# Regrouping the matmuls of a chunked RWKV-7 recurrence: keys' products as one block, outputs in two blocks

## The chip, the cores and the metric

The kernel runs on one core of a Trainium2 chip. Times are device microseconds (us) of that core; smaller is better. A time is given as the median of several runs. The profile is one further execution, taken by the hardware profiler: it lists every instruction of every engine with its start and length.

## The reference, cut to what matters

One layer of a hybrid decoder: a normed and modulated input goes through one projection, whose columns feed sparse attention (8 heads of 64) and an RWKV-7 time mix (8 heads of 64); both are concatenated and go through an output projection and a feed-forward network. There are 1024 prompt tokens and 8 sample tokens. The part that is changed here is the time mix of the prompt:

```python
def wkv7_step(S, inp):
    r, w, k, v, kk, a = inp
    sa = jnp.einsum('bhij,bhj->bhi', S, -kk)
    S = S * w[:, :, None, :] + sa[..., None] * (kk * a)[:, :, None, :] + v[..., None] * k[:, :, None, :]
    return S, jnp.einsum('bhij,bhj->bhi', S, r)
...
s_fin, ys = lax.scan(wkv7_step, s0.astype(jnp.float32), xs)
```

A state of 64 x 64 per head is carried from token to token; every token decays it, corrects it along one direction, adds value times key, and reads it with r. What comes out is group-normed, gets a bonus and a gate.

## The kernel before

The time mix is computed in chunks of C = 64 tokens. A unit of work is a pair of heads over QT = 256 tokens, so four chunks (HC = 4), and there are 16 units: unit n handles quarter q = n // 4 of the tokens and pair p = n % 4. A unit goes through four generators: `rw_prep` (operands), `rw_pre` (masked products within the chunks and the start of the inverses of the 32 x 32 diagonal blocks, which GpSimd computes), `rw_solve` (corrections, then the state chain) and `rw_norm` (outputs, group norm, gate). Each generator is cut by `yield` into steps, and `rwkv` gives each step a round: a unit starts every NR = 9 rounds, the steps of `rw_pre` come 9 to 14 rounds after the unit's start, those of `rw_solve` at RS = 27 to 35, those of `rw_norm` at RN = 36, 37, 39, 41 and 43. `rw_run` emits the steps sorted by round, so four or five units overlap.

The inverses of a unit go over DRAM: `rw_pre` writes the masked products `ga` to `d_l` (line 982), reads them back as `la` (986), GpSimd works on them in 31 pairs of instructions (1021 and 1023), `inv_back` writes `arr` to `d_t` (1034), behind the next unit's read of `la` on the SP queue, and reads the blocks `tt` (1038), which the first product of `rw_solve` (1052) uses.

At the end of `rw_solve` the state chain goes over the four chunks. For each head of the pair (e = 0 on partitions 0 to 63, e = 1 on 64 to 127) one matmul of the keys `bkt` with `uv` (line 1093, contraction over 128 partitions, 64 stationary columns, 64 moving columns) and one of the matrix `M` with the state `S` (line 1095, contraction over 64 partitions) add up in PSUM, and ScalarE scales the sum by `ec` into the next state (helper `SC`, line 51). The outputs in `rw_norm` add, for each chunk and head, the state part `Sa` by `rho` (line 1123, 64 partitions) and the chunk part `uv` by `gr` (line 1124, 128 partitions). In the first quarter (q = 0) the first chunk has no state, so the products with it fall away. All these are fp32 matmuls, which stand in the trace as two records each.

Attention of the prompt, the output projection of the first half of the tokens and the first feed-forward blocks are interleaved with the recurrence. The framework's planner sets the order on each engine ahead of time with a simulation of its own; on the chip every engine takes its instructions in that order.

Of the kernel before, what the change touches and what calls it, by code (L numbers as in the profile page):

```python
# [7 lines left out]
F32 = mybir.dt.float32  # L8
# [10 lines left out]
NS = 8  # L19
# [20 lines left out]
# rounds of the steps of a unit of the recurrence after its start; rounds from a unit's start to the next one's  # L40
# [19 lines left out]
# buffers: values; queries and keys; probabilities, transposed; keys split; queries loaded  # L60
# [13 lines left out]
class Ring:  # L74
    """tiles of several pools in turn"""
# [9 lines left out]
class Kern:  # L85
# [8 lines left out]
    # ------------------------------------------------------------------ constants  # L94
    def consts(self, ctx):
        nc, tc, I = self.nc, self.tc, self.I
        cp = self.cp
        with tc.tile_pool(name="tri0", bufs=1) as pp:
# [5 lines left out]
            self.tri_s = cp.tile([128, 128], F32, name="c_ts")     # col > row  # L104
# [25 lines left out]
        # parameters, one row of 128 each, transposed to columns  # L130
# [23 lines left out]
    # ------------------------------------------------------------------ adaLN modulation  # L154
# [17 lines left out]
    def mod_chunk(self, j, cw, wpool, tpool, keep=None):  # L172
        """columns cw*j.. of silu(c) @ w_ada; keep: SBUF tile [128, cw] taking the four partial rows"""
# [22 lines left out]
    # ------------------------------------------------------------------ norm 1, h transposed and split  # L196
# [5 lines left out]
    def norm_T(self, pool, mp, xp, fp):  # L202
        """norm 1 and its modulation; returns h transposed, hi, lo [128, KD, NT] (float32r)"""
# [55 lines left out]
    # ------------------------------------------------------------------ weights  # L259
    def wload(self, src, c0, n, wp):  # L260
        """src [1024, cols] -> hi, lo [128, KD, n], n <= 128"""
        return self.wtile(src, 0, c0, KD, n, wp)

    def mm_fm(self, ps, n, w, wc, m, h, t0, kd=KD):
        """ps[:m, :n] = W^T h (features by tokens), three passes"""
# [8 lines left out]
    def mm_tm(self, ps, n, h, t0, m, w, wc, kd=KD):  # L274
        """ps[:m, :n] = h^T W (tokens by features)"""
# [7 lines left out]
    # ------------------------------------------------------------------ RWKV, feature-major preparation  # L283
# [73 lines left out]
    def rsqrt(self, x, n, pool):  # L357
        """x [128, n] -> x ^ -0.5"""
# [12 lines left out]
    def rstd_tm(self, sq, blk, eps, floor, tp):  # L371
        """sq [128 = (2, 64), QT] -> (per token and half: sum with the weights of blk) ^ -0.5, tokens on partitions"""
# [11 lines left out]
    def rows_fm(self, ps, rn, n):  # L384
        """columns (token tile, half) of rn, tokens on partitions, as rows on all 64 partitions of each half"""
        for t in range(n):
            for h in range(2):
                self.nc.tensor.matmul(ps[64 * h:64 * h + 64, 128 * t:128 * t + 128],  # L388
                                      bc(rn[:, 2 * t + h:2 * t + h + 1], [128, 64]), self.ident, start=True, stop=True)

    def rw_prep(self, u, tp):
        """alpha, rho and kappa, beta of a pair of heads over QT tokens, per chunk; v; bonus"""
# [61 lines left out]
    # ------------------------------------------------------------------ indexer  # L454
    def idx_keys(self, h, wp, tp, sp, kp):
        """indexer keys, normalised, doubled over both halves of the partitions and split; weights per head"""
# [110 lines left out]
    def idx_select(self, tp, sp, smp):  # L567
        """scores -> 0 for the selected keys, -BIG for the others"""
# [17 lines left out]
        # keys under the middle: counted on DVE; on ACT as (under) - (over)  # L586
# [36 lines left out]
    def bis_open(self, lo, hi, w, t):  # L623
        """raise hi strictly over the maximum; w = hi - lo"""
# [7 lines left out]
    def bis_close(self, lo, hi, w, t):  # L632
        """the band of scores that rounding cannot tell from the threshold: [lo, hi]"""
# [7 lines left out]
    # ------------------------------------------------------------------ indexer of the sample tokens  # L641
    def smp_scores(self, tp, sp):
        nc, I = self.nc, self.I
        # page rows of 16 keys: row = page * 8 + sub; partition = (page of 16, sub of 8), column = (sequence, half)
# [14 lines left out]
        # head weights of every sequence on all partitions  # L659
# [7 lines left out]
        # head weights on partitions (eight times 16 heads), a column for each time  # L667
# [9 lines left out]
        # block-diagonal queries: column (key of two, head)  # L677
# [6 lines left out]
        # score of the token itself  # L684
# [15 lines left out]
        # cached keys  # L700
# [44 lines left out]
    def smp_prefix(self, x, rs, out, tp):  # L745
        """x [128, 16, 16] 0/1: inclusive count in the order (half, partition, key) of every sequence; totals"""
# [17 lines left out]
    def smp_select(self, tp, sp, dp):  # L764
# [56 lines left out]
        nc.vector.tensor_scalar(t, cnt, -1.0, TOPK + 0.5, op0=OP.mult, op1=OP.add)      # places left, + 0.5  # L821
# [11 lines left out]
        # slot of every selected key: the token itself, when selected, has slot 0  # L833
# [12 lines left out]
        # row of the key in the pools, selected ones only  # L846
# [35 lines left out]
    # ------------------------------------------------------------------ queries, keys, values (tokens on partitions)  # L882
    def split_sample(self, hi, lo, pool, name):
        """the sample tokens of a split operand as stationary columns: high parts at 0, low parts at 64"""
# [7 lines left out]
    def mm_smp(self, hs, w, wc, n, tp, out):  # L892
        """out [NS, n] = sample tokens times the n columns of w from wc"""
# [55 lines left out]
    # ------------------------------------------------------------------ RWKV recurrence: a pair of heads, QT tokens  # L949
    def rw_pre(self, u, tp, dp):  # L950
        """masked products within the chunks; starts the inverses"""
# [4 lines left out]
        # [.., 1, :]: V (tokens on partitions 0..63) and, later, the corrections without state (64..127);  # L956
        # [64.., .., 0, :]: what the state adds to the corrections
# [955 lines left out]
```

## Time and profile before

| | |
|---|---|
| runs | 2125.37, 2136.69, 2147.43 us; median 2136.69 |
| span of the profiled execution | 2141.3 us |
| TensorE matmul busy | 2033.1 us, 95% |
| VectorE busy | 1201.5 us, 56% |
| ScalarE busy | 815.7 us, 38% |
| GpSimd busy | 791.6 us, 37% |

The profiled execution's own time is its span, from the first instruction to the last. PE is TensorE's matmul, PEld its weight load, DVE VectorE, ACT ScalarE, POOL GpSimd, SP the engine that issues DMAs. Ends of matmuls are modelled, starts are measured; so a matmul's price is best read from the starts of two neighbours. A shape such as 128*64 128x64 says that the stationary operand has 128 rows and 64 columns, and that the operand named last has 128 partitions and 64 columns.

### The profile page before, as it was taken

The numbers are of one execution on the slowest core, as the hardware profiler recorded it, in microseconds if no ns is written. First come the engines' busy times: TensorE is split into PE (matmuls) and PEld (weight loads), VectorE is DVE, ScalarE is ACT, GpSimd is POOL, SyncE is SP. The second block draws the span as 40 slices with busy tenths as digits, with TensorE's granted clock in tenths as the row PEclk, the third lists the DMA queues.
The fourth block names the chain that finished last, engine by engine and source line by source line (L and its number), as shares of the span: only waits on it lengthen the run. The fifth ranks groups of instructions, "written<-read, shape, count | busy, mean of one in ns | idle before, by whom it ended". The sixth has DMA issues, their size and how long they took to land.

```text
span 2141.3 us, 38397 instructions
## 1 busy us (share of the span) xinstructions
PE 2033.1 (95%) x14794; PEld 1738.6 (81%) x14794; DVE 1201.5 (56%) x2904; ACT 815.7 (38%) x1650; POOL 791.6 (37%) x1381
## 2 busy tenths in 40 slices
PE   5999999889978999999999999999999999999998
PEld 3887888789964667777777887877788889999998
DVE  7777988997466554565565453575344463121215
ACT  5466676423222334455444332222322232222221
POOL 3411345332452246555635520101311244545452
PEclk8999999999988787999999899999999999999999
DMA  7311234233166654222113521443633234323333
GB/s 254 84 30 30 61 114 119 70 95 106 59 199 192 168 144 102 72 57 63 42 47 96 132 87 45 142 125 96 177 92 101 80 119 138 99 79 99 91 98 110
DMA packets 303206, 220.28 MB, mean 103 GB/s; under 512 B 67151, under 2 KB 281650, under 8 KB 303022
## 3 DMA queue, kind: packets, MB, share of 16 engines
q1 hardware_dynamic: 298140, 200.99, 32.5%
q0 software_dynamic: 4864, 16.78, 2.5%
q8 instruction: 117, 1.92, 0.4%
q14 instruction: 67, 0.55, 0.1%
q10 hardware_dynamic: 18, 0.04, 0.0%
HBM read 187.11 MB, written 30.13 MB: 101 GB/s over the span
## 4 chain that ended last, share of the span: by engine, by line
PE 68%; DMA 4%; DVE 3%; issue 1%; POOL 1%; ACT 0%; SPq 0%; DVEq 0%; POOLq 0%; ACTq 0%
PE ps L270 26%; PE ps L1657 11%; PE ps L1546 4%; PE ps L1255 2%; PE ps L1244 2%; PE ps L1124 2%; PE ps L972 1%; PE ps L1093 1%; PE ps L1123 1%; PE ps L1095 1%; PE ps L1224 1%; PE ps L388 1%; PE ps L183 1%; PE ps L1052 1%; PE ps L1065 1%
## 5 line engine op out<-in xcount | busy, mean ns | idle before, releaser
L1621 POOL TENSOR_TENSOR fl<-fr,fh 128x1024 fp32r<-128x1024 f32 (+1 forms) x109 | 264.2, 2429 | 323.4 <-ACT fh L1620 321.2
L1620 ACT ACTIVATE fh<-fr 128x1024 fp32r<-128x1024 f32 (+1 forms) x183 | 190.9, 1055 | 481.2 <-PE ps L270 268.4
L270 PE MATMUL ps<-h2hi,fh 128*128 128x264 f32 (+2 forms) x1056 | 336.3, 320 | 1.2 <-ACT fh L1620 1.2
L270 PE MATMUL ps<-h2lo,fh 128*128 128x264 f32 (+2 forms) x1056 | 336.2, 320 | 0.0
L270 PE MATMUL ps<-h2hi,fl 128*128 128x264 f32 (+2 forms) x1056 | 332.7, 320 | 0.6 <-DVE fl L1621 0.6
L270 PE MATMUL ps<-h1hi,fh 128*128 128x344 f32 (+1 forms) x752 | 250.1, 333 | 2.0 <-ACT rl L556 1.3
L270 PE MATMUL ps<-h1lo,fh 128*128 128x344 f32 (+1 forms) x752 | 246.9, 328 | 0.0
L270 PE MATMUL ps<-h1hi,fl 128*128 128x344 f32 (+1 forms) x752 | 246.4, 328 | 0.0
L270 PEld LDWEIGHTS ps<-h2hi,fh 128*128 128x128 f32 x1056 | 198.8, 188 | 16.5 <-ACT fh L1620 3.7
L1021 POOL TENSOR_TENSOR itmp<-la,arr 128x24 f32<-128x24 f32 (+23 forms) x496 | 131.2, 265 | 218.6 <-DMA la<-d_l 182.5
L270 PEld LDWEIGHTS ps<-h2hi,fl 128*128 128x128 f32 x1056 | 197.6, 188 | 15.4 <-DVE fl L1621 1.8
L270 PEld LDWEIGHTS ps<-h2lo,fh 128*128 128x128 f32 x1056 | 198.9, 188 | 13.6 <-issue 0.3
L1646 DVE TENSOR_TENSOR fa<-fa,ps 128x256 f32<-128x256 f32 (+1 forms) x66 | 33.8, 512 | 255.0 <-PE ps L270 255.0
L1657 PE MATMUL ps<-al,fh 128*128 128x512 f32 (+2 forms) x528 | 166.0, 320 | 3.2 <-DVE al L1648 3.2
L1668 DVE TENSOR_TENSOR acc<-acc,ps 128x512 f32<-128x512 f32 (+2 forms) x224 | 107.9, 514 | 99.5 <-PE ps L1657 99.4
L1657 PE MATMUL ps<-ah,fh 128*128 128x512 f32 (+2 forms) x528 | 157.5, 322 | 3.6 <-DVE fa L1646 1.9
L1657 PE MATMUL ps<-ah,fl 128*128 128x512 f32 (+2 forms) x528 | 160.5, 320 | 0.0
L270 PEld LDWEIGHTS ps<-h1hi,fh 128*128 128x128 f32 x752 | 143.8, 191 | 8.3 <-ACT rl L556 3.4
L1621 DVE TENSOR_TENSOR fl<-fr,fh 128x1024 fp32r<-128x1024 f32 x74 | 92.6, 1256 | 101.7 <-ACT fh L1620 100.2
L1023 POOL TENSOR_TENSOR arr<-arr,itmp 128x24 f32<-128x24 f32 (+23 forms) x496 | 132.5, 267 | 38.0
L270 PEld LDWEIGHTS ps<-h1lo,fh 128*128 128x128 f32 x752 | 143.6, 191 | 2.4 <-issue 2.1
L270 PEld LDWEIGHTS ps<-h1hi,fl 128*128 128x128 f32 x752 | 143.5, 191 | 2.5 <-issue 2.5
(937 smaller groups left out, 4382.3 us busy)
## 6 DMA issues: line engine op xcount, KB each, us to landing
fr<-in_w_ffn_gate_dram SPq DMA_DIRECT2D x44, 512.0 KB
fr<-in_w_ffn_up_dram SPq DMA_DIRECT2D x44, 512.0 KB
fr<-in_w_ffn_down_dram SPq DMA_DIRECT2D x44, 512.0 KB
fr<-in_w_in_dram SPq DMA_DIRECT2D x34, 512.0 KB
wr<-in_w_ada_dram SPq DMA_DIRECT2D x8, 1024.0 KB
la<-d_l SPq DMA_DIRECT2D x16, 512.0 KB
fr<-in_w_out_dram SPq DMA_DIRECT2D x16, 512.0 KB
d_x<-X SPq DMA_DIRECT2D x14, 512.0 KB
```

Of the source, the lines that this page charges most:

```text
L270: mm = nc.tensor.matmul(ps[:m, :n], a[:, k, wc:wc + m], b[:, k, t0:t0 + n], start=(k == 0 and i == 0), stop=(k == kd - 1 and i == 2))
L1021: ie.tensor_tensor(t3, bc(la[:, s, s + 1:][:, None, :], [128, nu, nt]), bc(arr[:, 0:nu, s:s + 1], [128, nu, nt]), op=OP.mult)
L1023: ie.tensor_tensor(arr[:, 0:nu, s + 1:], arr[:, 0:nu, s + 1:], t3, op=OP.subtract)
L1124: nc.tensor.matmul(ys, uv[:, c, e, 1, :], gr[:, c, e, :], start=not st, stop=True)
L1244: nc.tensor.transpose(ps[:, 128 * (l % 4):128 * (l % 4) + 128], P[e][:, 128 * l:128 * l + 128], ident)
L1255: nc.tensor.matmul(po[o, 0:128], vt[:, l, o], PT[e][:, 128 * (l % 4):128 * (l % 4) + 128], start=(l == 0), stop=(l == i))
L1546: nc.tensor.matmul(p3[:, t, :], a[:, k, ts], b[:, k % 4, :], start=(k == 0 and n == 0), stop=(k == KD - 1 and n == 2))
L1620: nc.scalar.activation(hi, raw, AF.Copy)
L1621: self.loe.tensor_tensor(lo, raw, hi.bitcast(F32), op=OP.subtract)
L1646: nc.vector.tensor_tensor(a, a, pu[:, :n], op=OP.mult)
L1657: nc.tensor.matmul(ps[:, :n], a[:, 0, 128 * o:128 * o + 128], b[:, c:c + n], start=(i == 0), stop=(i == 5))
L1668: nc.vector.tensor_tensor(a, a, ps[:, :n], op=OP.add)
```

## The change

In `rw_solve` the products M and rho are computed in one step. In the next step the keys' products of all four chunks run as one block of 8 matmuls into one PSUM tile, and VectorE multiplies them by `ec` into the new tile `bu`. The state chain keeps only the products with M; VectorE scales each and adds the chunk's part of `bu` in one instruction. The first chunk is in that same step, so that the chain ends one step earlier. In `rw_norm` the state parts of all chunks come first and the chunk parts of all chunks after them, as one accumulation over the PSUM tile. The rest of the diff takes comments out.

```diff
     def rw_solve(self, u, tp):
...
         nc.vector.tensor_tensor(M, c4(ps[:, :QT]), bc(self.id2[:, None, :], [128, HC, C]), op=OP.add)
-        yield
         ps = new()
...
         nc.vector.tensor_tensor(rho, rho, c4(ps[:, :QT]), op=OP.add)
+        yield
+
+        bu = tp.tile([128, HC, C], F32, name="bu", bufs=2)
+        ps = new()
+        for c in range(HC):
+            for e, o in enumerate(E2):
+                nc.tensor.matmul(ps[o, 64 * c:64 * c + 64], bkt[:, c, o], uv[:, c, e, 1, :], start=True, stop=True)
+        nc.vector.tensor_tensor(bu, c4(ps[:, :QT]), bc(ec[:, :, None], [128, HC, C]), op=OP.mult)
+
         Sa = u.Sa = tp.tile([128, HC, C], F32, name="Sa", bufs=2)
         S = None
         if u.q:
             S = Sa[:, 0, :]
             nc.scalar.activation(S, self.sfin[:, u.p, :], AF.Copy)
         for c in range(HC):
+            Sn = Sa[:, c + 1, :] if c < HC - 1 else self.sfin[:, u.p, :]
+            if S is None:
+                nc.scalar.activation(Sn, bu[:, c, :], AF.Copy)
+            else:
+                ps = self.psc.tile([128, 512], F32, name="ps")
+                for e, o in enumerate(E2):
+                    nc.tensor.matmul(ps[o, 0:64], M[o, c, :], S[o, :], start=True, stop=True)
+                nc.vector.scalar_tensor_tensor(Sn, ps[:, 0:64], ec[:, c:c + 1], bu[:, c, :], op0=OP.mult, op1=OP.add)
+            S = Sn
             yield
-            Sn = Sa[:, c + 1, :] if c < HC - 1 else self.sfin[:, u.p, :]
-            ps = self.psc.tile([128, 512], F32, name="ps")
-            for e, o in enumerate(E2):
-                nc.tensor.matmul(ps[o, 0:64], bkt[:, c, o], uv[:, c, e, 1, :], start=True, stop=S is None)
-                if S is not None:
-                    nc.tensor.matmul(ps[o, 0:64], M[o, c, :], S[o, :], start=False, stop=True)
-            SC(nc, Sn, ps[:, 0:64], ec[:, c:c + 1])
-            S = Sn
         if u.q == T // QT - 1:
             self.wkv_out(u.p, tp)
...
     def rw_norm(self, u, tp):
...
         ps = new()
+
+        c0 = 0 if u.q else 1
+        E2 = [(e, slice(64 * e, 64 * e + 64)) for e in range(2)]
+        for c in range(c0, HC):
+            for e, o in E2:
+                nc.tensor.matmul(ps[o, 64 * c:64 * c + 64], Sa[o, c, :], rho[o, c, :], start=c == c0, stop=False)
         for c in range(HC):
-            for e in range(2):
-                o = slice(64 * e, 64 * e + 64)
-                ys = ps[o, 64 * c:64 * c + 64]
-                st = u.q or c
-                if st:
-                    nc.tensor.matmul(ys, Sa[o, c, :], rho[o, c, :], start=True, stop=False)
-                nc.tensor.matmul(ys, uv[:, c, e, 1, :], gr[:, c, e, :], start=not st, stop=True)
+            for e, o in E2:
+                nc.tensor.matmul(ps[o, 64 * c:64 * c + 64], uv[:, c, e, 1, :], gr[:, c, e, :], start=False, stop=c == HC - 1)
         nc.scalar.activation(y, ps[:, :QT], AF.Copy)
```

## Rows read from the trace of the kernel before

**Rows 1.** Stretches: us, busy PE PEld DVE ACT POOL, granted clock, DMA, GB/s

```profile
850.00:1150.00 300.00, 299.81 (x2876) 226.74 (x2876) 172.51 (x658) 144.55 (x351) 158.46 (x600) 0.98 0.21 54
1150.00:1200.00 50.00, 47.97 (x436) 37.31 (x432) 25.55 (x73) 21.68 (x47) 28.63 (x97) 0.83 0.57 159
1200.00:1350.00 150.00, 148.50 (x1103) 122.78 (x1102) 68.61 (x147) 47.43 (x98) 29.42 (x93) 0.95 0.26 80
```

**Rows 2.** The chain of waits, 780 to 1350 us, shares by line

```profile
by line: PE ps L1546 8.3%; PE ps L1255 6.9%; PE ps L270 6.2%; PE ps L1124 6.0%; PE ps L1244 5.4%; PE ps L1093 5.4%; PE ps L1123 5.3%; PE ps L1095 5.2%; PE ps L972 5.0%; PE ps L1224 4.0%; PE ps L388 3.5%; PE ps L1052 3.3%; PE ps L1065 3.3%; 
```

**Rows 3.** TensorE's groups by form, 780 to 1350 us: busy, mean, idle before

```profile
L1124 PE MATMUL ps<-gr,uv 128*64 128x64 f32 x256 | 43.2, 259 | 0.0
L1093 PE MATMUL ps<-uv,bkt 128*64 128x64 f32 x256 | 42.4, 248 | 2.8 <-ACT Sa L51 2.8
...
L1074 PE MATMUL ps<-bkt,uv 64*64 64x64 f32 x256 | 13.1, 226 | 0.2
```

**Rows 4.** TensorE's timeline, outputs of a first-quarter unit: start, us, instruction

```profile
875.85 0.34 PE L1124 MATMUL ps<-gr,uv 128*64 128x64 f32 x4
876.11 0.32 PE L1123 MATMUL ps<-rho,Sa 64*64 64x64 f32 x2
876.37 0.33 PE L1124 MATMUL ps<-gr,uv 128*64 128x64 f32 x2
```

**Rows 5.** TensorE's timeline, 1012.8 to 1018 us

```profile
1012.86 0.60 PE L997 MATMUL ps<-c_id,ar 128*64 128x128 f32 x4
1013.29 0.51 PE L377 MATMUL ps<-c_bm,t 128*128 128x2 f32 x4
...
1016.39 0.66 PE L388 MATMUL ps<-c_id,rn 128*64 128x128 f32 x8
1016.98 0.68 PE L1080 MATMUL ps<-gr,uv 64*64 64x64 f32 x16
1017.59 0.66 PE L1244 MATMUL ps<-c_id,P 128*128 128x128 f32 x4
```

**Rows 6.** VectorE's groups by form, 780 to 1350 us

```profile
L367 DVE SCALAR_TENSOR_TENSOR rq_a<-rq_y,rn 128x4 f32<-128x4 f32 x87 | 13.9, 161 | 1.4
...
L1137 DVE SCALAR_TENSOR_TENSOR y<-y,prm,ps 128x256 f32<-128x256 f32 x16 | 7.6, 478 | 12.6 <-PE ps L388 12.3
...
L1075 DVE TENSOR_TENSOR M<-ps,c_id 128x256 f32<-128x256 f32 x16 | 6.7, 421 | 3.2 <-PE ps L1074 2.8
```

**Rows 7.** Line 51, the state's scaling on ScalarE, and its idle before it

```profile
L51 ACT ACTIVATE Sa<-ps,ec x48: 293/314/316, 796.7 to 1328.0; 128x64 f32<-128x64 f32 x48
L51 ACT ACTIVATE sfin<-ps,ec x16: 314/314/316, 802.4 to 1333.4; 128x64 f32<-128x64 f32 x16
...
  PE ps L1095: 73.5, 49
```

**Rows 8.** Timelines of TensorE, GpSimd and SP: one unit's inverses

```profile
1007.56 1.16 PE L972 MATMUL ps<-ar,bk 64*128 64x128 f32 x8
...
1020.01 0.48 POOL L1021 TENSOR_TENSOR itmp<-la,arr 128x31 f32<-128x31 f32 x1 [7.88 <-DMA la<-d_l]
...
1040.77 0.20 POOL L1023 TENSOR_TENSOR arr<-arr,itmp 128x4 f32<-128x4 f32 x1
...
1042.73 0.63 SPq L1034 DMA_DIRECT2D d_t<-arr  x1
1049.35 1.73 SPq L1038 DMA_DIRECT2D tt<-d_t  x4
...
1060.64 1.09 PE L1052 MATMUL ps<-X,tt 64*64 64x128 f32 x16
```

**Rows 9.** Line 972 from 850 to 1110 us: 16 records per unit

```profile
L972 PE MATMUL ps<-ar,bk x144: 272/272/373, 855.8 to 1106.0; 64*128 64x128 f32 x144
```

**Rows 10.** ScalarE's timeline ahead of the output projection

```profile
1186.43 1.06 ACT L1517 ACTIVATE h2hi<-fr 128x1024 fp32r<-128x1024 f32 x1 [4.46 <-DMA fr<-d_mix]
...
1192.72 1.06 ACT L1620 ACTIVATE fh<-fr 128x1024 fp32r<-128x1024 f32 x1 [1.45 <-DMA fr<-in_w_out_dram]
```

## The prediction

> **What bounds the kernel now.** The recurrence lies between about 790 and 1335 us, so I read that part only. First the busy time by stretch [rows 1]: TensorE is busy 299.8 of 300 us from 850 to 1150, 48.0 of 50 and 148.5 of 150 after it, while VectorE has 172.5, ScalarE 144.6 and GpSimd 158.5 of the 300. The granted clock is 0.98 there, so nearly all of it runs at 2.4 GHz. Then the chain of waits from 780 to 1350 [rows 2]: it names TensorE's own lines and hardly anything else, and the four lines that the change regroups, 1093 and 1095 (state chain), 1123 and 1124 (outputs), hold 5.4 + 5.2 + 5.3 + 6.0 = 21.9% of 570 us, 124.8 us. Third, the groups by form [rows 3]: line 1093 waited for the state for 2.8 us in all. So TensorE is not kept waiting; a microsecond taken off its queue here is a microsecond of the end, until something else becomes late. Behind 1350 us the kernel is feed-forward, bound by TensorE too, and is only moved forward.
>
> Why these lines are dear is seen in the groups and the timeline. Line 1124 takes 43.2 us for 256 records, line 1074, with the same 64 moving columns and as many records, 13.1 us [rows 3]. (One fp32 matmul leaves two records.) In the timeline [rows 4] the output's matmuls alternate between a stationary tile of 128 rows (1124) and one of 64 rows (1123), and each change starts 0.26 us after the one before: 875.85, 876.11, 876.37. The first row is telling: four records, both heads, took the same 0.26 us as two, because both heads have the same tile shape. Where the shape stays [rows 5], line 1080 runs 16 records in 17.59 - 16.98 = 0.61 us, 0.076 us per matmul instead of 0.26.
>
> **The change part by part.** The number of matmuls stays: 128 keys' products, 120 state products, 120 state parts of outputs, 128 chunk parts, 496 in all. Only their order and grouping change.
>
> Removed: the alternation. 496 x 0.26 = 129 us agrees with the 124.8 us of the chain, which I take.
>
> Put in its place, per row durations: the keys' products, 16 blocks of 8 matmuls, all 128 x 64. The trace has no block of that shape with 64 moving columns. Bounds: from below line 1080's 0.61 us [rows 5]; from above no overlap of the two heads, priced below. Line 388 is nearer, because it has the same tile shape and alternating heads with 128 moving columns: 8 records in 0.59 us. Line 1124's four records in 0.26 us show the overlap at 64 columns. So 0.61: 16 x 0.61 = 9.8 us. Chunk parts of the outputs: the same shape, 16 x 0.61 = 9.8 us. State parts: 64 x 64, 12 blocks of 8 and 4 of 6 (first quarter), 12 x 0.61 + 4 x 0.49 = 9.3 us. State chain: a pair of heads per chunk stands alone between other work, 60 x 0.26 = 15.6 us. Sum 44.5 us; saved 124.8 - 44.5 = 80 us.
>
> A page speaks against the 32 blocks of 128 rows. The row: four records in the time of two [rows 4]. The Trainium skill, "TensorE: Matmul & The Clock Gate", section Part 3, The mechanism, says that a weight load overlaps matmuls in flight only where the row group differs; here both heads use all rows. By the row the blocks cost 0.61 us, by the rule about what the second rival below says; the row contradicts it for two heads.
>
> Evictions: the keys' products add 16 VectorE multiplications, near line 1075 (0.42 us) [rows 6], 6.7 us. The scaling of the state moves from ScalarE (64 of 0.31 us, 20 us [rows 7]) to VectorE; the trace has no such operation at 64 columns; its bounds are the 0.16 us of 4 columns and the 0.48 us of 256 [rows 6]; by the columns 0.24 us, 60 x 0.24 = 14 us. VectorE gets 21 us more in 545, which its idle 42% [rows 1] covers; uncovered it is 21 us on the path. Behind these operations on VectorE stand the masked scores and copies that attention's next matmuls need. I take 5 us, from 0 to 21. The four copies that stay on ScalarE are free: it loses more than it gets.
>
> Moved: M and rho now stand in one round, the chain starts in the fifth and ends one round before the unit's last. The outputs start at the same round, so they gain slack. No DMA is moved past anything by the code; only the last state transposition keeps its place. The extra PSUM tile per unit lies in a ring of three that its VectorE eviction empties in 0.4 us: nothing, or a wait of that length 16 times, 7 us.
>
> What is late next, first: the inverses. For one unit [rows 8] line 972 starts at 1007.6, GpSimd works from 1020.0 to 1041.0, the write back is issued at 1042.7, the read at 1049.4 to 1051.1, and the solve (1052) starts at 1060.6: 53.1 us, of which 9.6 lie behind the issue of the last read. Nine units' line 972 lie between 855.8 and 1106.0 [rows 9], 31.1 us per unit. The chain in the program has fixed rounds, so the 53.1 us shrink with the period: 31.1 - 5.0 (80/16) = 26.1, and 53.1 x 26.1 / 31.1 = 44.6 us. The latency needs 43.5 us up to the last read's issue, 41.7 when the write back no longer stands behind the next unit's read (1.8 us after GpSimd's end), and its landing, which no row gives: between 0 and the 7.0 us that write back and its wait take (1042.7 to 1049.4, rounded up). So a unit stalls 0 to 4 us, 12 units 0 to 48. The read is of small blocks, so I take 8 us in sum.
>
> Second: before the output projection TensorE has only recurrence work, while ScalarE waits for loads (4.46 and 1.45 us, up to 1192.7 [rows 10]). What is saved there is partly lost: 0 to 10, I take 6.
>
> Sum: 80 - 5 - 8 - 6 = 61 us. The profiled span, 2141.3 us, becomes 2080; it is 4.6 us over the runs' median, 2136.7, and inside their range. From the median: 2076 us. Ends of the known costs: 80 saved without losses, 2057, a little below for parts at the lower clock (0.83 from 1150 to 1200), where a matmul that no longer alternates saves more; and 2097 if the planner, which orders each engine's queue by its own simulation, leaves every pair of heads alone: 248 x 0.26 = 64.5, saved 60, less 19.
>
> **The rivals.** One: the inverses become the bound. For: after the sum only 0 to 3 us of slack per unit are left. Against: 9.6 us are there now. At the far end 80 - 5 - 6 - 48 = 21 us, 2116; in the middle 2105.
>
> Two: heads with the same rows don't overlap in a long block. Line 997 [rows 5], one head's columns only, takes (13.29 - 12.86) / 4 = 0.107 us per record; 16 records 1.7 us and the 0.15 us of a change: 1.87, 1.26 more than above, 32 x 1.26 = 40 us. Then 80 - 40 - 19 = 21 us, 2116. Against it: line 388's eight records and line 1124's four. It is the rule of the page above.
>
> Three, slower: VectorE takes over the waiting. ScalarE waited 73.5 us, 49 times, in its 64 scalings for the chain's matmuls [rows 7], harmlessly. On VectorE a wait holds scores and copies behind it. If each of 60 waits of 1.5 us (73.5 / 49) ends on TensorE, 90 + 21 - 80 = 31 us slower, 2168. It decides once VectorE has no idle time left: from 850 to 1350 it has 500 - 267 = 233 us [rows 1]; less 80 and 21, 132 remain, more than 90. So it needs bad order, not load.
>
> Four: the change does not do what it says, since it is accumulating onto a place just written that costs 0.26 us, not the shape. Against: in rows 4 the next head's first product, which opens a new place, costs 0.26 too. 2137.
>
> **How the numbers follow.** The forecast with its own range (2050 to 2097) 0.68; rival one, 2097 to 2118, 0.15; two 0.05; three 0.07; four 0.05. Runs of this kernel spread by 0.5% to either side, so about 1% (2115 to 2158) is what can be told from no change. Faster: 0.68 + 0.12 + 0.03 = 0.83; within: 0.03 + 0.02 + 0.05 = 0.10; slower 0.07. Range 2048 to 2112, with what lies over 2112 left out.
>
> **What would show it.** After the change the keys' and chunk parts' lines should show 16 records in about 0.61 us and their groups about 12 us each instead of 43; four lines under 50 us in all. The period of line 972 should be 26 us, with TensorE no longer at 100%. Right in mechanism but small: waits of line 1052 for the inverse's read, or of masked scores on the state's VectorE lines. Wrong: blocks of 16 records still near 1.9 us, or still cut up by other shapes.

## The result, and the profile after

The changed kernel takes 2085.05 us (median of 4 runs, 2079.03 to 2093.12), the kernel before 2138.28 us beside it: ratio 0.973, 95% interval 0.9696 to 0.9764. The forecast was 2076 us, a ratio of 0.9716; its range held the time. The profiled span fell from 2141.3 to 2078.6 us, by 62.7 us, with the same mean granted clock of 0.955 in both. Ratios leave out an execution that is more than 1.5% above the fastest of its kernel; the one such below is the profiled execution of e1.

The busy time by stretch, columns as in [rows 1]:

```profile
850.00:1150.00 300.00, 280.57 (x3180) 217.81 (x3176) 200.63 (x741) 143.81 (x331) 186.95 (x685) 0.95 0.29 78
1150.00:1200.00 50.00, 49.31 (x469) 46.62 (x468) 23.61 (x44) 19.34 (x47) 20.74 (x57) 1.00 0.34 96
1200.00:1350.00 150.00, 137.22 (x888) 107.83 (x888) 75.41 (x167) 41.53 (x65) 12.23 (x27) 0.95 0.30 96
```

TensorE was busy 299.8 of the 300 us from 850; now it is 280.6. It does more work in the same stretch (3180 matmul records for 2876) and still waits 19 us. So the regrouping moved the bound a little: TensorE is no longer the only limit. The chain of waits from 780 to 1350 us says the same:

```profile
by line: PE ps L270 11.8%; PE ps L1264 6.0%; PE ps L1666 5.8%; PE ps L1253 5.1%; PE ps L1555 4.2%; DMA d_t<-arr 3.8%; PE ps L972 3.3%; PE ps L1233 2.9%; issue 2.7%; POOL itmp L1021 2.5%; PE ps L388 2.4%; DMA la<-d_l 2.4%; DMA qt<-out_dram 2
```

None of the four regrouped lines is among the leading ones, where they had 21.9% [rows 2]. New is the path of the inverses: the write-back (`d_t<-arr`), the elimination on GpSimd (1021) and its load (`la<-d_l`), 8.7% together.

TensorE's groups by form, 780 to 1350 us. The keys' block is line 1087, the chain's product 1102, the state parts 1130 and the chunk parts 1133:

```profile
L1102 PE MATMUL ps<-Sa,M 64*64 64x64 f32 x240 | 21.3, 245 | 6.5 <-DVE Sa L1103 5.9 <-ACT Sa L1098 0.6
L1130 PE MATMUL ps<-rho,Sa 64*64 64x64 f32 x240 | 15.8, 240 | 0.0
L1133 PE MATMUL ps<-gr,uv 128*64 128x64 f32 x256 | 12.6, 237 | 0.0
L1074 PE MATMUL ps<-bkt,uv 64*64 64x64 f32 x256 | 12.5, 234 | 1.2 <-ACT uv L1067 1.0
L1087 PE MATMUL ps<-uv,bkt 128*64 128x64 f32 x256 | 11.8, 232 | 4.7 <-DVE rho L1080 4.0 <-ACT bkt L1005 0.7
```

The two lines with 128 rows cost 12.6 and 11.8 us where they had 43.2 and 42.4 [rows 3], and now cost about the same as line 1074. The mean length of one record hardly moved (259 to 237 ns and 248 to 232 ns), and its end is modelled. What fell is the distance between starts, and that is read from the timeline:

```profile
1197.83 0.69 PE L1087 MATMUL ps<-uv,bkt 128*64 128x64 f32 x16 [0.69 <-ACT bkt L1005]
1198.45 0.27 PE L1102 MATMUL ps<-Sa,M 64*64 64x64 f32 x2
...
1202.23 0.33 PE L1102 MATMUL ps<-Sa,M 64*64 64x64 f32 x4 [0.26 <-DVE Sa L1103]
1202.40 0.28 PE L1130 MATMUL ps<-rho,Sa 64*64 64x64 f32 x4
1202.95 0.33 PE L1102 MATMUL ps<-Sa,M 64*64 64x64 f32 x4 [0.27 <-DVE Sa L1103]
1203.12 0.28 PE L1130 MATMUL ps<-rho,Sa 64*64 64x64 f32 x4
1203.33 0.69 PE L1133 MATMUL ps<-gr,uv 128*64 128x64 f32 x16
1203.95 0.30 PE L1112 MATMUL ps<-c_id,sfin 128*64 128x128 f32 x1
```

Sixteen records of the keys' block take 1198.45 - 1197.83 = 0.62 us, sixteen of the chunk parts 0.62 us too, against 0.26 us for two when they alternated [rows 4]. A pair of the chain in front of state parts of its own shape costs 0.17 us. Added up over the whole timeline, from the start of each record of the four lines to TensorE's next start and without idle time ("by starts" from here on), they fell from 126.6 to 47.7 us.

Where TensorE now waits, 780 us to the feed-forward's first product (us in total, times, longest):

```profile
PE ps L1597 <- ACT ox L1590: 9.5, 1, 9.5
PE ps L1102 <- DVE Sa L1103: 5.9, 6, 3.8
PE ps L450 <- DVE xr L447: 5.1, 6, 1.4
PE ps L1087 <- DVE rho L1080: 4.0, 1, 4.0
PE ps L1555 <- ACT fh L1629: 3.5, 1, 3.5
PE ps L1052 <- DMA tt<-d_t: 2.2, 3, 1.7
```

The longest is behind the output projection, in front of norm 2's transpositions. Its history stands in the timeline of VectorE, GpSimd, SP and TensorE:

```profile
1199.07 0.73 DVE L1560 TENSOR_TENSOR ox<-ox,oy 128x512 f32<-128x512 f32 x1
1206.88 1.05 POOL L200 TENSOR_TENSOR ors<-ors,c_mh 128x4 f32<-128x4 f32 x1
1206.95 0.63 SPq L1034 DMA_DIRECT2D d_t<-arr  x1
1208.25 0.53 SPq L1575 DMA_DIRECT2D d_x<-ox  x1
1216.91 1.42 DVE L1588 TENSOR_SCALAR ox<-ox,ors 128x1024 f32<-128x1024 f32 x2 [9.96 <-DMA d_x<-ox]
1218.10 3.67 PE L1597 MATMUL ps<-c_id,ox 128*128 128x128 f32 x16 [9.47 <-ACT ox L1590]
```

`ox` is complete at 1199.80. It is stored (1575) and then scaled in place (1588, 1590) by the root of its row sums (200). SP issues the store only at 1208.25, since the write-back of an inverse (1034) stands ahead of it and waits for GpSimd; the root stands behind the same inverse on GpSimd. Neither the store nor the root is a part of the recurrence; they only share its queues.

The state's new step on VectorE, by form and by who waits for it:

```profile
L1103 DVE SCALAR_TENSOR_TENSOR Sa<-ps,ec,bu 128x64 f32<-128x64 f32 x44 | 12.1, 276 | 2.4 <-PE ps L1102 2.4
L1088 DVE TENSOR_TENSOR bu<-ps,ec 128x256 f32<-128x256 f32 x16 | 6.7, 417 | 0.0
L1103 DVE SCALAR_TENSOR_TENSOR sfin<-ps,ec,bu 128x64 f32<-128x64 f32 x16 | 4.5, 282 | 13.6 <-PE ps L1102 13.2
...
  PE ps L1102: 15.6, 12
...
  PE ps L1102: 5.9, 6
```

VectorE stood 15.6 us, 12 times, for the chain's matmuls, where ScalarE had stood 73.5 us, 49 times [rows 7]; TensorE in turn stood 5.9 us, 6 times. Line 972 gives the period of a unit:

```profile
L972 PE MATMUL ps<-ar,bk x141: 272/272/373, 839.0 to 1059.9; 64*128 64x128 f32 x141
```

Nine units again [rows 9]: less the 1.4 us between the first and the last record of one unit, (1059.9 - 839.0 - 1.4) / 8 = 27.4 us, from 31.1.

### The profile page after: what moved, and what is told of

It reads as the page before. It is cut to its first block, busy times and chain, and to the rows that moved or that the text cites. A ratio compares the mean times of both kernels' runs of the same rounds, so it can differ in the third digit from the quotient of the medians.

```text
span 2078.6 us, 38421 instructions
## 1 busy us (share of the span) xinstructions
PE 1946.7 (94%) x14794; PEld 1677.5 (81%) x14794; DVE 1225.0 (59%) x2980; ACT 796.7 (38%) x1590; POOL 793.4 (38%) x1381
## 4 chain that ended last, share of the span: by engine, by line
PE 61%; DMA 7%; DVE 3%; POOL 2%; issue 1%; SPq 1%; ACT 1%; DVEq 0%; ACTq 0%; POOLq 0%
PE ps L270 27%; PE ps L1666 11%; PE ps L1555 3%; PE ps L1264 2%; PE ps L1253 2%; PE ps L1233 1%; PE ps L972 1%; DMA qt<-out_dram 1%; DMA d_t<-arr 1%; PE ps L183 1%; PE ps L388 1%; POOL itmp L1021 1%; PE ps L1052 1%; PE ps L1234 1%; PE ps L1059 1%
```

## The experiments

Theory: the price of the old order is the change of tile shape between neighbouring matmuls on TensorE, and what the regrouping saves is partly given back in waits for queues that the recurrence shares with other work. Rivals: accumulation onto a place just written is the price, not the shape; the inverses have become the bound; VectorE has.

Each run is set against runs of the kernel before on the same chip. "Idle" is TensorE's from 780 to 1290 us (510 us less its busy time there), "clock" the mean granted one over the profiled run, and "span x clock" the profiled span times it, a rough way to take different clocks out. Span and clock are known of nearly every run; the last column gives the mean clock and the mean of span times clock over the runs behind a ratio. (For the kernel before it is the range over its runs on four chips, 11 or 19 on each.)

| run | ratio to before, 95% | idle, us | span, us | clock | span x clock, us | all runs: clock, span x clock |
|---|---|---|---|---|---|---|
| before | 1 | 5.3 | 2141.3 | 0.955 | 2045 | 0.948 to 0.952, 2043 to 2044 |
| changed | 0.973, 0.9696 to 0.9764 | 38.2 | 2078.6 | 0.955 | 1985 | 0.955, 1990 |
| e1 chain alone | 0.9954, 0.991 to 0.9997 | 27.4 | 2161.4 | 0.933 | 2017 | 0.945, 2022 |
| e2 outputs alone | 0.9779, 0.9704 to 0.9854 | 13.1 | 2110.5 | 0.951 | 2007 | 0.957, 2014 |
| e3 outputs in pairs | 0.9795, 0.9721 to 0.987 | 29.1 | 2104.2 | 0.948 | 1995 | 0.948, 1996 |
| e4 outputs alternating | 0.9932, 0.9893 to 0.9971 | 27.1 | 2141.4 | 0.941 | 2015 | 0.946, 2020 |
| e5 store by ScalarE | 0.9712, 0.9675 to 0.9749 | 31.9 | 2091.9 | 0.951 | 1989 | 0.953, 1992 |
| e6 VectorE's step in two | 0.9709, 0.9667 to 0.9752 | 33.0 | 2100.2 | 0.948 | 1991 | 0.953, 1994 |
| e7 half the inverse | 0.9754, 0.9712 to 0.9796 | 32.4 | 2090.5 | 0.954 | 1994 | 0.950, 1992 |
| e8 the same, before | 1.0144, 1.0092 to 1.0196 | 21.5 | 2179.3 | 0.938 | 2044 | 0.937, 2044 |
| e9 store by columns | 0.9735, 0.9686 to 0.9784 | 36.4 | 2103.8 | 0.949 | 1997 | 0.950, 1994 |
| e10 and steps later | 0.9751, 0.9707 to 0.9795 | 27.0 | 2098.2 | 0.952 | 1998 | 0.952, 1998 |
| e11 and write-back by GpSimd | 0.9717, 0.9679 to 0.9756 | 36.3 | 2087.0 | 0.955 | 1993 | 0.952, 1993 |
| e12 and root on VectorE | 0.9748, 0.9697 to 0.98 | 30.0 | 2092.2 | 0.949 | 1986 | 0.951, 1988 |

The profile of e1 ran at a mean granted clock of 0.933, its nine other runs at 0.938 to 0.953; so its span, its idle time and its times by starts are not set against the others' without the clock.

### The change in halves: e1 and e2

e1 keeps the new `rw_solve` and puts the old loop of the outputs back:

```diff
-        for c in range(c0, HC): ...state parts...
-        for c in range(HC): ...chunk parts...
+        for c in range(HC):
+            for e in range(2):
+                ...state part, then chunk part of one head...
```

> The keys' block and the short state chain alone; the outputs alternate between state and chunk parts as before. Theory (every change of the stationary tile's shape costs about 0.2 us on TensorE): the two chain lines take about 28 us of TensorE's time instead of 63, the two output lines stay at 66; TensorE no longer waits for nothing, so about four fifths of the 35 us reach the end: 2138 becomes about 2110. Rival (the gain is the state chain's shorter latency, not TensorE's time): this run alone has nearly the whole gain, about 2088.

e2 keeps the old `rw_solve` and takes the new order of the outputs (the same diff the other way, on the kernel before).

> The outputs in two blocks alone; the state chain as before. Theory (shape changes): output lines take about 25 us instead of 66, chain lines stay at 63; the end comes about 35 us earlier, near 2104. Rival (latency of the state chain): no gain, 2138, since the outputs start only after the chain.

The halves gain 0.5% (barely clear of nothing) and 2.2%, which add up to the whole change's 2.7%. By starts, the four lines take 102.7 us in e1 and 87.4 in e2, of 126.6: savings of 24 and 39 us. In e1 the chain lines fell from 60.5 to 26.2 us, as expected, but the output lines, whose order is that of the kernel before, rose from 66.1 to 76.5: 206 of their 496 records lie in stretches at the lower clock level (1.2 GHz), 65 in the kernel before.

In time, against the kernel before on the same chip (2150.22 us), e2's median is 43 us lower, where 35 were expected; e1's is 7 us lower (10 by the ratio), where 28 were expected. Much of the difference is the clock, whose mean was 0.950 for the kernel before, 0.945 for e1 and 0.957 for e2. Span times clock fell by 20 us in e1 and by 29 in e2, 49 of the whole change's 53. Why the clock differs between the kernels is open. The profiles' idle time, 27.4 us in e1 and 13.1 in e2, points to the new solve as the part that makes TensorE wait; with e1's at another clock that is not shown.

### Shape or accumulation: e3 and e4

Both edit the outputs of the changed kernel alone; the products are the same and so is the number of them. e3 goes chunk by chunk: the state parts of both heads, then the chunk parts of both.

```diff
-        for c in range(c0, HC): ...state parts of both heads...
-        for c in range(HC): ...chunk parts of both heads...
+        for c in range(HC):
+            ...state parts of both heads, then chunk parts of both heads...
```

> As the changed kernel, but the outputs go chunk by chunk: both heads' state parts, then both heads' chunk parts, so 7 or 8 runs of four records instead of two blocks. Theory (shape changes): each run costs 0.26 us, output lines take 16 x 8 x 0.26 = 33 us instead of 25 (a third matter: half the changes of the kernel before); the end is 5 to 10 us later than the changed kernel, 2090 to 2095. Rival (what costs 0.26 us is adding to a place that the matmul just before has written): here two matmuls lie between, no, one lies between, and both are done with, so about as fast as the blocks, 25 us and 2085.

e4 changes the shape at every matmul, but a chunk part never follows the state part of its own place: it is the part two chunks further on.

```diff
+        st = [(c, e, o) for c in range(c0, HC) for e, o in E2]
+        ck = [((c + 2) % HC, e, o) for c in range(HC) for e, o in E2]
+        for i, (c, e, o) in enumerate(ck):
+            if i < len(st): mm(state part, *st[i])
+            mm(chunk part, c, e, o)
```

> As the changed kernel, but the outputs alternate between a state part and a chunk part that belongs to another chunk, so that the shape changes with every matmul, and none adds to a place that its neighbour has just written. Theory (shape changes): output lines take 0.26 us per matmul again, 62 to 66 us instead of 25, and the end is about 30 us later than the changed kernel, near 2115. Rival (accumulation onto a place just written): as fast as the blocks, 25 us and 2085.

TensorE's timeline of e4, then of e3:

```profile
877.98 0.32 PE L1132 MATMUL ps<-rho,Sa 64*64 64x64 f32 x2
878.24 0.33 PE L1132 MATMUL ps<-gr,uv 128*64 128x64 f32 x2
878.49 0.33 PE L1132 MATMUL ps<-rho,Sa 64*64 64x64 f32 x2
```

```profile
849.47 0.33 PE L1132 MATMUL ps<-rho,Sa 64*64 64x64 f32 x4
849.73 0.34 PE L1132 MATMUL ps<-gr,uv 128*64 128x64 f32 x4
850.00 0.33 PE L1132 MATMUL ps<-rho,Sa 64*64 64x64 f32 x4
```

The change costs 0.26 us in both, whether one matmul (two records) or two stand between changes, and in e4 nothing accumulates onto a place just written. That settles it: shape, not accumulation. The output lines together take 69.6 us by starts in e4 (0.140 us per record) and 35.6 in e3 (0.072), against 23.4 in the changed kernel (0.047) and 66.1 before. The rival four of the prediction falls. The Trainium skill, "TensorEngine Tiling (Array Packing)", Key Properties, says that a change of the tiling mode drains TensorE; the runs fit that and give a price, 0.26 us, but none shows apart that the time goes into a drain.

The time follows. Against the changed kernel e4 has 46 us more on these lines and is 2.0% (43 us) slower by ratio, where about 30 were expected; e3 has 12 us more and is 0.65% (14 us, with an interval of 16 to either side) slower, where 5 to 10 were expected. The times that the expectations name can't be set beside the measured ones, since the kernel before is 12 us slower on this chip (2150 for 2138). With the clock taken out the two come to 2020 and 1996 us against 1990, 30 and 5 us more. So the rest of e4's loss is a lower clock (0.946 for 0.955), whose cause is open.

### VectorE's step made longer: e6

```diff
-                nc.vector.scalar_tensor_tensor(Sn, ps[:, 0:64], ec[:, c:c + 1], bu[:, c, :], op0=OP.mult, op1=OP.add)
+                nc.vector.tensor_scalar(Sn, ps[:, 0:64], ec[:, c:c + 1], None, op0=OP.mult)
+                nc.vector.tensor_tensor(Sn, Sn, bu[:, c, :], op=OP.add)
```

> The changed kernel with VectorE's one step behind each pair of the state chain (0.276 us) done in two, a product and a sum: 60 instructions more on VectorE, each estimated at 0.2 us from the 0.15 to 0.28 us of its other 64-column steps, so 12 us more of VectorE and 0.2 us more in each of 60 links of the chain. Theory (VectorE's step is mostly covered by TensorE's other work; in the changed kernel TensorE waits for it in 6 of 60 links, 5.9 us): 2 to 4 us slower, 2087 to 2090. Rival (VectorE's step has become the link that sets the end, the third rival of the prediction): 12 us or more slower, 2097 to 2105.

VectorE's groups by form in this run (780 to 1290 us), and TensorE's waits:

```profile
L1103 DVE TENSOR_SCALAR Sa<-ps,ec 128x64 f32<-128x64 f32 x40 | 11.1, 278 | 5.1 <-PE ps L1102 5.0
L1104 DVE TENSOR_TENSOR Sa<-Sa,bu 128x64 f32<-128x64 f32 x40 | 9.6, 240 | 0.4
...
PE ps L1052 <- DMA tt<-d_t: 11.4, 4, 7.0
PE ps L1102 <- DVE Sa L1104: 4.6, 5, 1.8
```

Each link got 0.24 us longer, VectorE did some 14 us more, and the ratio is 0.9709: no cost that can be measured. TensorE waited for the step in 5 links, 4.6 us, as before. Rival three is refuted for this size: VectorE's load and the length of a link don't set the end. (The order of all engines was planned anew around the longer step, so this says what the step costs in a kernel planned for it. The waits moved with it: the one for the inverse's read grew from 2.2 to 11.4 us, and the one in front of norm 2 is gone.)

### Inverses: e7, e8 and e10

```diff
-        for s in range(31):
+        for s in range(16):
```

> The changed kernel with 16 of the 31 elimination steps of each inverse on GpSimd; the second half of the elimination is left out, so the inverses are incomplete. Each inverse takes some 10 us less. Theory (the inverses are the next thing late after the change, in the waits of L1052 and in SyncE's queue, where the write-back holds other transfers): 8 to 12 us faster than the changed kernel, 2073 to 2077. Rival (the inverses are covered as before): 0 to 3 us, 2082 to 2085.

> The kernel before with the same half of the elimination left out. Both theories expect 0 to 3 us here, as the inverses had 4 to 10 us to spare: ratio 0.998 to 1.0. A gain as large as that of the changed kernel with half the elimination would say that the inverses cost the same before and after, and that the change doesn't make them later.

The windows 780 to 1290 us of the kernel before, of the changed one, of e7 and of e8 (columns as in [rows 1]):

```profile
780.00:1290.00 510.00, 504.72 (x4624) 392.43 (x4619) 274.37 (x947) 225.60 (x539) 254.89 (x927) 0.94 0.29 76
```

```profile
780.00:1290.00 510.00, 471.83 (x4886) 374.41 (x4885) 310.21 (x1047) 220.50 (x494) 251.72 (x902) 0.94 0.30 83
```

```profile
780.00:1290.00 510.00, 477.61 (x4932) 377.44 (x4931) 311.80 (x1063) 223.64 (x503) 137.72 (x480) 0.94 0.32 84
```

```profile
780.00:1290.00 510.00, 488.52 (x4373) 375.14 (x4372) 254.92 (x900) 213.19 (x511) 135.80 (x485) 0.88 0.28 72
```

GpSimd's work fell by 114 us in e7 (251.7 to 137.7), and the time not at all: 0.9754 against 0.973, and 1992 against 1990 us with the clock taken out. My expectation, 8 to 12 us faster, was wrong, and the theory that the inverses' arithmetic is the next bound falls with it. e10 says the same from the other side: with all steps behind the inverse one round later (on top of e9, below)

```diff
-RS = (27, 28, 29, 30, 31, 32, 33, 34, 35)
-RN = (36, 37, 39, 41, 43)
+RS = (28, 29, 30, 31, 32, 33, 34, 35, 36)
+RN = (37, 38, 40, 42, 44)
```

with CUT and CUT2 108 instead of 107.

> The same, and every step of a unit behind its inverse one round later (the lists RS and RN and the cuts CUT and CUT2 one higher). After the change a unit takes 27 us in place of 31, so the steps behind the inverse reach it earlier. Theory (the inverses are covered, as the run with half of each left out says): no gain from more room, 0 to 4 us slower than the column stores alone, as the last unit ends a round later. Rival (the inverses are late): 4 to 10 us faster than the column stores alone, ratio 0.964 to 0.967.

The ratio stays (0.9751 against e9's 0.9735). The feed-forward's first product came 38 us earlier than in e9 (1214.0 against 1251.6 us) and the recurrence ended 42 us later (1370.1 against 1328.2): work was moved past a mark, not saved.

e8 came out on the wrong side of both theories: with less work on GpSimd the kernel before was 1.4% slower, in all its four runs. The clock gives the difference: in the windows the granted clock of the stretch is 0.88 and not 0.94, over the four runs it is 0.933 to 0.939 (the kernel before on this chip 0.942 to 0.956), and span times clock, 2044 us, is that of the kernel before. What in its order brought the lower clock is open; its TensorE idles more (21.5 us against 5.3), but the changed kernel idles more still at 0.94.

### The wait behind the output projection: e5, e9, e11 and e12

e5 moves one DMA issue; the order of matmuls stays as it was:

```diff
-        nc.sync.dma_start(x2, X)
+        nc.scalar.dma_start(x2, X)
```

> The changed kernel with one transfer moved: the store of the scaled residual (ox to d_x, 2 MB) is issued by ScalarE instead of SyncE; TensorE's, VectorE's and GpSimd's order stays as it is. In the changed kernel that store is issued at 1208.25 us, behind the inverse's write-back on SyncE's queue (1206.95), though ox was ready at 1199.80; the scaling of ox in place waits for it until 1216.9 and TensorE stands 9.5 us before L1597. Theory (the queue holds the store): issued at about 1200.8, landed at about 1209.5, so TensorE's wait at L1597 falls to 1 to 3 us and the time by 6 to 8 us, to 2077 to 2079. Rival (the wait is only handed on, to the next wait of ScalarE or of the feed-forward's weights): the wait at L1597 falls, the time doesn't, 2083 to 2087.

e9 replaces it by one store per column block, in the loop of the output projection:

```diff
+            nc.scalar.dma_start(x2[:, :, cs], X[:, :, cs])
```

> The changed kernel with the residual stored in four column blocks by ScalarE, each as soon as its block of the output projection is added, in place of one store of 2 MB by SyncE behind all four. In the run with the store on ScalarE the wait of TensorE before L1597 fell from 9.5 to 1.5 us and the stretch from the output projection's first product to the feed-forward's first product from 89.5 to 84.9 us, while the whole time stayed within its spread (0.9712 against 0.973 of the kernel before). Theory (the store is the wait): wait below 1 us, that stretch 82 to 85 us, ratio to the kernel before 0.968 to 0.971. Rival (the wait is handed on): stretch 87 to 90 us, ratio 0.973.

e11 adds to e9 the write-back on GpSimd's queue (`nc.gpsimd.dma_start` in `inv_back`).

> The column stores, and the inverse's write-back (arr to d_t) issued by GpSimd, which computes it, in place of SyncE. In the changed kernel SyncE stands 24.4 us in 8 waits for GpSimd before this transfer, and every transfer queued behind it stands too. Theory (SyncE's order at the write-back is a part of the waits that the change brought; TensorE's waits between 780 us and the feed-forward's first product are 36.9 us after and 5.3 before): these waits fall by 5 to 10 us and the ratio is 0.964 to 0.968. Rival (SyncE's waits are covered but for the residual's store, or GpSimd pays as much for the issue): same as the column stores alone, within 4 us.

e12 adds to e9 the root of the row sums on VectorE:

```diff
-        self.rstd_col(rs[:, :nt + smp], rs[:, :nt + smp], D, 1e-6)
+        nc.vector.tensor_scalar(rs[:, :nt + smp], rs[:, :nt + smp], 1.0 / D, 1e-6, op0=OP.mult, op1=OP.add)
+        self.rsqrt(rs[:, :nt + smp], nt + smp, tp)
```

> The column stores, and the root of norm 2's row sums taken by VectorE's own iteration (eleven short instructions of 0.15 to 0.20 us, 2 us in all) in place of one power on GpSimd (L200, 1.05 us). With the column stores alone that power began at 1239.18 us, when GpSimd had finished the inverse in front of it, though its operand had been ready for 6.5 us by ScalarE's wait, and TensorE stood 6.1 us before L1597; in the kernel before GpSimd had been waiting 12.0 us for that operand. Theory (the inverse holds GpSimd's queue, and after the change it does so when norm 2 needs it): the wait at L1597 falls below 2 us, the stretch from the output projection's first product to the feed-forward's first product from 82.2 to 76 to 78 us, ratio to the kernel before 0.966 to 0.972. Rival (the next transfer or eviction takes its place): that stretch stays at 80 to 83 us, ratio 0.9735.

| | before | changed | e5 | e9 | e11 | e12 |
|---|---|---|---|---|---|---|
| wait in front of the transpositions of norm 2, us | - | 9.5 | 1.5 | 6.1 | 7.5 | 1.5 |
| output projection's first product to the feed-forward's, us | 81.2 | 89.5 | 84.9 | 82.2 | 83.3 | 76.6 |

That the wait went from 1.5 us in e5 back to 6.1 in e9, where the store is out of the way altogether, showed the second half of the cause. The timeline of VectorE, GpSimd and TensorE in e9:

```profile
1232.91 0.16 DVE L199 TENSOR_SCALAR ors<-ors 128x4 f32<-128x4 f32 x1
1239.18 1.05 POOL L200 TENSOR_TENSOR ors<-ors,c_mh 128x4 f32<-128x4 f32 x1
...
1240.27 1.41 DVE L1588 TENSOR_SCALAR ox<-ox,ors 128x1024 f32<-128x1024 f32 x2 [6.01 <-POOL ors L200]
...
1241.47 3.67 PE L1597 MATMUL ps<-c_id,ox 128*128 128x128 f32 x16 [6.10 <-ACT ox L1590]
```

The root's operand is ready at 1233.07; GpSimd takes it up at 1239.18, at the end of an inverse. In the kernel before GpSimd had been waiting for the operand for 12.0 us. With the root on VectorE the wait is 1.5 us again, now for the store:

```profile
PE ps L1598 <- ACT ox L1591: 1.5, 1, 1.5
```

and the stretch is 12.9 us shorter than in the changed kernel, as expected of it. In e11 the store by columns stands, the root still waits for GpSimd and TensorE for it (7.5 us); SP's place behind GpSimd was not the cause there. The theory of e11 fails on the whole stretch too: TensorE's waits from 780 us to the feed-forward's first product are 36.2 us, in e9 36.4.

The wait in front of norm 2 belongs to one order of the queues, not to the change as such: e6, which leaves store and root as they are in the changed kernel, has none there, e10, which is e9 one round later, has none, and e7 has 0.9 us.

In the whole time none of the four shows a gain: 0.9712, 0.9735, 0.9717 and 0.9748 against 0.973, each within about 0.5%. For e5 and e9, gains of 5 to 7 us would be within that; but with the clock taken out the means of e5, e9 and e11, 1992 to 1994 us, are no lower than the changed kernel's 1990, so that the gain may as well have been handed on to a later wait. For e12 it isn't enough: 12.9 us would be 0.967, just outside its interval. In its profile attention ends at 1128.2 us, in the changed kernel's at 1105.4, though the edit lies behind that point. Of these 23 us, 17 are time lost at the lower clock up to there (90.5 us lost against 73.4, which is the clock's missing share added up) and 6 are waits (101.4 against 95.0); attention's end less both is 936.3 and 937.0 us. So the profiled run of e12 was late before it came to the edit. Its six runs had a lower clock too, 0.951 on the mean against 0.955; with the clock taken out they stand at 1988 us, a hint of a gain at most. Why it was lower stays open. No version here is shown to beat the changed kernel.

## Why the prediction was right

The time came within 0.5% of the forecast, and by the mechanism that it named: the alternation of shapes was the price. Two of its terms were off, the losses too small and a saving on other lines left out, and that they nearly cancel is luck.

**The saving** was sized well. Predicted 124.8 - 44.5 = 80 us on the four lines; by starts 126.6 - 47.7 = 79. The parts: keys' products 10.5 us (predicted 9.8), chunk parts 11.3 (9.8), state parts 12.1 (9.3), chain 13.8 (15.6). The chain's pairs are cheaper than 0.26 us because some stand beside products of their own shape, and the state parts dearer because they do not stay one block (1202.23, 1202.40, 1202.95, 1203.12: a pair of the chain, then two heads' state parts, then the next pair). The measured price of a shape change is the 0.26 us of [rows 4]. It depends on the clock: by starts an output matmul of the kernel before takes 0.25 us on the mean at 2.4 GHz and 0.39 us in the stretches at 1.2 GHz.

**Rival two** is refuted: the blocks with 128 rows take 0.62 us, not 1.87. The rule of the Trainium skill behind it ("TensorE: Matmul & The Clock Gate", Part 3, The mechanism) differs from the measurement for two heads in two halves of the columns, at least as the prediction drew it, and the measurement decides.

**The losses** were sized at 19 us; TensorE's idle time from 780 to 1290 us rose by 38.2 - 5.3 = 33, over the whole span by 118.1 - 93.6 = 24.5, as it fell elsewhere. Term by term, for the stretch:

- VectorE's evictions, 5 taken, bounds 0 to 21: the waits of lines 1102, 450 and 1087 for VectorE are 5.9 + 5.1 + 4.0 = 15.0 us. The instructions themselves were right (0.28 us each, estimated 0.24; `bu` 0.417 for 0.42). e6 shows that it isn't their length.
- The inverses, 8 taken, bounds 0 to 48: line 1052 waits for the read 2.2 us. The unit's period is 27.4 us, 1.3 more than predicted; the six units whose line 972 starts from 839.0 to 969.6 start line 1052 43.1 to 47.5 us later, where 44.6 was predicted. So the solve came about as near as forecast, and the read was there in time but for 2.2 us. But 9.5 us more stand in front of norm 2, where the inverse holds GpSimd's queue and through it SP's. This is the place that the prediction did not see: it had counted no DMA or step as moved past the inverse, and that is true in the code; the inverse moved in time.
- In front of the output projection, 6 taken: 3.5 us (line 1555).

Their sum is 30, of 33.

**What the sum had left out.** Over the whole span TensorE's other lines, 13801 records in both kernels, take 1898.7 us by starts, 1906.3 before: 8 us less. The time lost at the lower clock is 3.5 us less (93.6 for 97.1), which may be a part of it; the rest is open. So 79 + 8 - 24.5 = 62 of the 62.7 us.

Two small slips of the working change nothing: the upper end of the forecast's own range comes to 2096 by its terms, not 2097, and the write-back and its wait took 6.6 us, not 7.0.

**Rival one** (the inverses bound, 2105 to 2116) did not happen, and e7 and e10 show that half the elimination or a round more of room gives nothing. **Rival three** did not happen (e6). **Rival four** is refuted (e4).

**The signs it named** were there: 16 records in 0.62 us, groups of 11.8 and 12.6 us, four lines under 50 us by starts (61.5 by groups, where modelled ends overlap), TensorE at 94% from 850 to 1150 us, a period of 27.4 us where 26 was forecast, and waits at line 1052 and at the chain's VectorE step.

## What to carry to other kernels

Where small matmuls of two tile shapes alternate, read the distance between starts, not the mean duration: here 0.26 us per change against 0.04 to 0.05 us per record inside a block of one shape, and regrouping was worth 2.7% without one matmul less. Put every such line in a table of starts before sizing; the rest of the gain depends on what else stands in the in-order queues. When an engine that was 100% busy gets slack, look for steps of quite other work that share a queue with the next longest chain (here norm 2's root and its store behind an inverse): whether they wait depends on when the chain passes, and another order of the queues moves or removes the wait. Here gains of under half a per cent showed in the stretch that they belong to and not in the whole time. Set times side by side only with the granted clock of the same runs beside them, and sum by starts over the whole span: a stretch that ends at a mark takes work moved past the mark for work saved.

## What the runs showed of the hardware

Two heads in two column halves, each with all 128 rows, run as fast as 64 x 64 tiles: 16 records in 0.62 us against 0.61 [rows 5]. A change of shape costs the same 0.26 us whether one matmul or two of a shape stand between changes; at the lower clock level an alternating matmul takes 0.39 us from start to start for 0.25. And the granted clock is a term of its own: between 780 and 1290 us it was 0.94 in the kernel before and 0.88 in e8, which does less work, and that difference (0.06 x 510 = 31 us) is the size of its loss.
